# Order of the squares of x, the 64-row block product of two triangular inverses, and the queue of their transfers

## The chip, the cores and the metric

The kernel runs on one core of a Trainium2 chip. The metric is the device time of one execution in microseconds (us); for each kernel several executions are timed and the median is given. The engines of the core each work through their own list of instructions in order: PE (TensorE, matrix products), DVE (VectorE), ACT (ScalarE), POOL (GpSimd) and SP (SyncE, which here only starts transfers). ACT and POOL start transfers as well, and a transfer that an engine starts stands in that engine's list.

## The reference

One layer on x of 512 rows and 1024 columns, in float32: an RMS norm, one wide input projection, four parallel mixers (gated DeltaNet, RG-LRU, S5, RWKV-7), their output projections merged by sigmoid gates, an output projection, a squared-ReLU MLP and a last norm.

```python
h = _rmsnorm(x, norm1_g)
proj = h @ w_in
p_gdn, p_lru, p_s5, p_rwkv, p_gate = _split(proj, (GDN_COLS, LRU_COLS, S5_COLS, RWKV_COLS, GATE_COLS))
ys = (_gdn_mixer(p_gdn, ...), _rglru_mixer(p_lru, ...), _s5_mixer(p_s5, ...), _rwkv7_mixer(p_rwkv, ...))
for i in range(N_BRANCH):
    term = jax.nn.sigmoid(gate_logits[:, :, i]) * (ys[i] @ w_branch[i])
    merged = term if merged is None else merged + term
x = x + (merged @ w_out).astype(x.dtype)
h2 = _rmsnorm(x, norm2_g)
x = x + (jnp.square(jax.nn.relu(h2 @ mlp_w1)) @ mlp_w2).astype(x.dtype)
```

Two of the mixers are recurrences over time. The kernel computes both in chunks of 64 steps, and each needs the inverses of 32 unit triangular 64x64 matrices (4 heads by 8 chunks). These two sets of inverses are what the change is about: one for RWKV-7 (tiles whose names end in r) and one for the gated DeltaNet (names that end in g).

## The kernel before, in words

**Products.** A weight unit is 128 x 1024 numbers (512 KB). `unit` starts its transfer into a tile `raw` from SP's queue; ACT copies it to a rounded tile `hi` (L117), DVE computes `lo` = raw - hi (L120). `gemm` then makes 24 matrix products of 512 columns, three for each of eight slices of x: hi by the high part of x, hi by its low part, lo by its high part (L114). There are two tiles of `hi` and of `lo` and four of `raw`, so weights run a few units ahead of PE. The results stand in PSUM tiles called `acc`.

**Head.** `norm1` makes the high and low parts of each of the eight slices of x, scaled by the norm's weight: ACT writes the high part (L117, "split"), DVE the low part (L129). It then calls `norm_stat`, where ACT squares each slice (L117), DVE adds the squares up (L120), and PE sums over rows (`ssa`) and spreads the reciprocal root (`rsa`). While all this starts, PE runs `WARM` products of no use (`warm`); each counts as two passes in the trace.

**Order of the work.** A list of steps is given priorities, and a scheduler places every instruction on its engine's list by a timeline that it simulates. So a change of one step's instructions moves others around it. What the scheduler has written, the engines then execute in order, each instruction waiting for what it needs.

**The inverse.** `tri_inverse(nt, tf, nm)` runs once for r and once for g. `nt` holds 32 matrices of 64 rows. (1) It is written to memory in two transfers (L446) and read back in two (L450) with the 16x16 diagonal blocks laid out one to a partition. (2) DVE inverts those blocks in a loop of 15 steps of two operations each (L120, L459). (3) The inverses go to memory in four transfers, plain and transposed (L466), and come back in four (L470) as the tiles `a0t` and `tf`. Of the twelve transfers SP's queue starts six and ACT's six. (4) PE joins blocks of 16 to blocks of 32: `zp` is 64 products with a 16-row operand, ACT moves it to `zt` with one operation, `t1p` and `t2p` are 64 and 32 products, and ACT and DVE copy and add the results into place (L492, L494, L495). (5) PE joins blocks of 32 to blocks of 64 with `z2p` and `z3p`, 32 products each. The tile `tf` is then used by the recurrences.

**Around it.** `gdn_b` prepares the DeltaNet's decays: DVE copies the tile `pkT` out of PSUM, SP writes it to memory as `gscr` (L847), SP reads it back four times (L859, one tile that ACT then takes the exponential of), and ACT reads it back four more times (L853). `s5_y` reads the tile `scy` back with 16 transfers in ACT's list (L1344), ahead of a product called `glu`. The recurrences are chains of small products, `r`, `us`, `sn` and `oT`, between which ACT (L690, L691) and DVE (L124) move the results.

Of the kernel before, what the change touches and what calls it, by code (L numbers as in the profile page):

```python
# [11 lines left out]
ACT = mybir.ActivationFunctionType  # L12
# [85 lines left out]
RW0 = 1800  # L98
GATE0 = 2824
@with_exitstack  # L100
def trunk(ctx, tc, order, xT, wall, w8, prm, big, cst, gfr, out):
# [14 lines left out]
    def act(o, i, f, scale=1.0, bias=0.0):  # L116
        A.activation(out=o, in_=i, func=f, scale=scale, bias=bias)  # L117
# [181 lines left out]


    count = {"u": 0, "raw": 0}
    third = []

    def place(key):
        if key not in order:
# [10 lines left out]
    def unit(key, more=None, chain=None):  # L316

        u = count["u"]
        count["u"] += 1
        with priority(100 * u - (30000 if u else 50000)):  # L320
            k = u % (DEEP + len(third) // 2)
            if k < DEEP:
                hi, lo = (wp.tile([128, 1024], R, tag=f"{e}{k}", name=f"{e}{u}") for e in ("hi", "lo"))
            else:
                hi, lo = third
            if chain is None:
                raw = load(key)
            else:
                raw = chain
                (G if more is None else nc.sync).dma_start(out=raw, in_=wall[place(key)], **({"accum_op": ADD} if more is None else {}))  # L330
            if more is not None:
                G.dma_start(out=raw, in_=wall[place(more)], accum_op=ADD)
            act(hi, raw, ACT.Copy)
            tt(V, lo, raw, hi.bitcast(F), SUB)
        return v3(hi, 8), v3(lo, 8)

    def gemm(o, w, rh, rl, nk=8, k0=0, first=True, last=True):
        wh, wl = w
        n = 0
# [65 lines left out]

    def norm1():

        for k in range(8):
            split_g(xs[k], "g1", k, xgh[:, k, :], xgl[:, k, :])
        N1["rs"] = norm_stat(xs, "a")  # L410
        fr(xt)

    def proj(col):

        o = pa("acc")
        gemm(o, unit(("in", col)), xgh, xgl)
# [25 lines left out]
    def tri_inverse(nt, tf, nm):  # L442

        scr = tri_scr[nm]
        for par in range(2):
            (nc.sync, nc.scalar)[par].dma_start(  # L446
                out=flat(scr, 4160 * par, [[64, 64], [8320, 16], [1, 64]]), in_=nt[64 * par:64 * par + 64])
        nb, tn, tn2, tmp = (t1(n + nm) for n in ("nb", "tn", "tm", "tp"))
        for qe in range(2):
            (nc.sync, nc.scalar)[qe].dma_start(  # L450
                out=v3(nb, 16)[64 * qe:64 * qe + 64], in_=flat(scr, 1040 * qe, [[2080, 64], [64, 16], [1, 16]]))
# [12 lines left out]
        for qe in range(2):  # L464
            for s, t in ((0, tn3), (1, tm3)):
                (nc.sync, nc.scalar)[s].dma_start(  # L466
                    out=flat(tri_scr[nm, s], 1040 * qe, [[2080, 64], [64, 16], [1, 16]]), in_=t[64 * qe:64 * qe + 64])
        for par in range(2):
            for s, t in ((0, a0t), (1, tf)):
                (nc.sync, nc.scalar)[s].dma_start(  # L470
                    out=t[64 * par:64 * par + 64], in_=flat(tri_scr[nm, s], 4160 * par, [[64, 64], [8320, 16], [1, 64]]))
        fr(tn, tn2)

        zt, t11t, z2 = t1("zt" + nm), t2("t11t" + nm), t2("z2" + nm)
        zt3, t11, z23 = v3(zt, 16), v3(t11t, 16), v3(z2, 16)
        zp, t1p = ps("zp" + nm), ps("t1p" + nm)
        zp3 = v3(zp[:, 0:256], 16)
        t1p3, t2p3 = v3(t1p[:, 0:256], 16), v3(t1p[:, 256:512], 16)
        for x in range(16):
            for b in range(4):  # L480
                r0, c0 = 32 * b, 32 * (b % 2)
                mm(zp3[r0:r0 + 32, x, :], nt[r0:r0 + 16, x, c0:c0 + 32], a0t[r0:r0 + 16, x, c0:c0 + 16])
        act(zt, zp[:, 0:256], ACT.Copy, c_("hm")[:, 0:1])
        for x in range(16):
            for b in range(4):
                r0, c0 = 32 * b, 32 * (b % 2)
                mm(t1p3[r0:r0 + 16, x, :], zt3[r0:r0 + 32, x, :], tf[r0:r0 + 32, x, c0 + 16:c0 + 32])
                if b % 2 == 0:
                    mm(t2p3[r0:r0 + 32, x, :], tf[r0:r0 + 32, x, 0:32], zt3[r0:r0 + 32, x, :])
        for b in range(4):  # L490
            r0, c0 = 32 * b, 32 * (b % 2)
            A.copy(out=tf[r0:r0 + 16, :, c0 + 16:c0 + 32], in_=t1p3[r0:r0 + 16])  # L492
            if b % 2 == 0:
                tt(V, t11[r0:r0 + 32, :, 0:16], t2p3[r0:r0 + 32], a0t[r0:r0 + 32, :, 0:16], ADD)  # L494
                A.copy(out=t11[r0:r0 + 32, :, 16:32], in_=a0t[r0:r0 + 32, :, 16:32])  # L495
        fr(zt, t0t)

        z2p, z3p = ps("z2p" + nm), ps("z3p" + nm)
        z2p3, z3p3 = v3(z2p, 16), v3(z3p, 16)
        for x in range(16):  # L500
            for par in range(2):
                r0 = 64 * par
                mm(z2p3[r0 + 32:r0 + 64, x, :], nt[r0:r0 + 32, x, 32:64], t11[r0:r0 + 32, x, :])
        for par in range(2):
# [1324 lines left out]
```

## Time and profile before

| | |
|---|---|
| median of three runs | 880.21 us |
| the three runs | 877.97, 880.77, 880.21 us |
| the profiled execution's own time | 878.37 us |
| its span in the trace | 876.6 us |
| busy: PE, DVE, ACT, POOL | 852.6, 547.4, 427.2, 26.0 us |
| mean granted clock of TensorE | 0.988 |

A row of a timeline gives start and duration in us, the engine, the line of the kernel, the operation, and output and input by the program's names (tiles c, c0, c1a, c1b, c2, c3 are named storage places that many values pass through); in square brackets stands how long that engine had been idle just before, and what ended it. "x28" merges 28 instructions. A row of the waits gives the engine that waited, the tile, what it waited for, the total in us, the number of waits and the longest. A row of the windows gives, for a stretch from A to B, the busy time of PE, of its weight loads (PEld), DVE, ACT and POOL with their instructions, then the granted clock of TensorE, the busy share of the transfer engines and GB/s.

### The profile page before, as it was taken

Reading aid. Unit: us, or ns where it says so; the run is one execution under the profiler, and the core shown is the slowest. Engines: PE = TensorE matmul, PEld = TensorE weight load, DVE = VectorE, ACT = ScalarE, POOL = GpSimd, SP = SyncE. Lnnn points to the kernel's source line nnn. Section 1 sums busy time; section 2 is a strip of 40 time slices with the busy share of each in tenths; the row PEclk is TensorE's granted clock in tenths of the full one; section 3 lists DMA queues with packets and bytes.
Section 4 is the critical chain, followed back from the end, with each engine's and each line's share of the span. In section 5 each row is a group of like instructions: output and inputs, shape, how many; then the busy total and the mean of one; then the engine's idle time right before and its main releaser. Section 6 shows DMA issues by size and latency. Waiting matters only on the chain.

```text
span 876.6 us, 13021 instructions
## 1 busy us (share of the span) xinstructions
PE 852.6 (97%) x5175; PEld 683.9 (78%) x5175; DVE 547.4 (62%) x974; ACT 427.2 (49%) x600; POOL 26.0 (3%) x38
## 2 busy tenths in 40 slices
PE   8999999998999899999999999999999999999996
PEld 6777777777767677777888788888888888888885
DVE  6899796993676347845645652454437553868553
ACT  8735557954532254433523333765545443644433
POOL 1000000000000000000000000000100110010000
PEclk9999999998999899999999999999999999999998
DMA  8433345455365643344232232556676877463302
GB/s 298 134 114 104 109 117 111 105 148 147 111 182 155 163 144 111 107 119 136 73 106 99 75 130 96 192 145 174 164 195 165 239 170 194 164 137 104 120 25 96
DMA packets 79293, 119.97 MB, mean 137 GB/s; under 512 B 42544, under 2 KB 49392, under 8 KB 79216
## 3 DMA queue, kind: packets, MB, share of 16 engines
q1 hardware_dynamic: 51968, 100.40, 35.5%
q0 software_dynamic: 3456, 12.58, 8.5%
q10 hardware_dynamic: 23808, 6.16, 3.3%
q8 instruction: 40, 0.66, 0.3%
q14 instruction: 21, 0.17, 0.1%
HBM read 103.79 MB, written 13.17 MB: 133 GB/s over the span
## 4 chain that ended last, share of the span: by engine, by line
PE 80%; DVE 7%; DMA 6%; ACT 4%; issue 2%; ACTq 1%; SPq 1%; DVEq 0%
PE acc L114 24%; PE facc L114 20%; PE dacc L114 17%; PE oacc L114 5%; PE bacc L114 5%; DVE c L120 2%; DMA c1a<-scrg 1%; ACT c L117 1%; DVE lo L120 1%; PE s L114 1%; DVE c1a L120 1%; DVE c L129 1%; ACT L117 1%; DMA c1a<-gscr 1%; DMA scrg<-c1a 1%
## 5 line engine op out<-in xcount | busy, mean ns | idle before, releaser
L114 PE MATMUL acc<-c,hi 128*128 128x512 f32 x864 | 279.1, 401 | 3.1 <-DVE c L129 2.5
L117 ACT ACTIVATE hi<-raw 128x1024 fp32r<-128x1024 f32 x113 | 119.5, 1058 | 214.8 <-PE facc L114 73.5
L120 DVE TENSOR_TENSOR lo<-raw,hi 128x1024 fp32r<-128x1024 f32 x113 | 138.1, 1223 | 117.9 <-ACT hi L117 117.8
L114 PEld LDWEIGHTS acc<-c,hi 128*128 128x128 f32 x864 | 162.4, 191 | 43.2 <-DVE c L129 5.0
L114 PE MATMUL acc<-c,lo 128*128 128x512 f32 x432 | 175.1, 406 | 2.0 <-DVE lo L120 2.0
L114 PE MATMUL facc<-c,hi 128*128 128x512 f32 x336 | 103.4, 389 | 0.0
L114 PEld LDWEIGHTS acc<-c,lo 128*128 128x128 f32 x432 | 82.3, 190 | 21.9 <-DVE lo L120 3.1
L117 ACT ACTIVATE c<-c 128x512 f32<-128x512 f32 (+5 forms) x101 | 63.9, 638 | 19.3 <-DVE c L120 12.3
L114 PEld LDWEIGHTS facc<-c,hi 128*128 128x128 f32 x336 | 63.1, 188 | 13.0
L120 DVE TENSOR_TENSOR c<-c 128x16 f32<-128x16 f32 (+8 forms) x125 | 65.3, 537 | 5.1 <-ACT c L117 4.6
L114 PE MATMUL facc<-c,lo 128*128 128x512 f32 x168 | 65.5, 390 | 0.0
L114 PE MATMUL facc<-c,c1a 128*128 128x512 f32 x264 | 62.8, 391 | 0.0
L114 PE MATMUL dacc<-hi,c 128*128 128x512 f32 x176 | 57.4, 389 | 0.0
L117 ACT ACT_TABLE_LOAD x41 | 52.6, 1283 | 9.6 <-DMA c<-scu 3.7
L114 PEld LDWEIGHTS facc<-c,c1a 128*128 128x128 f32 x264 | 49.3, 188 | 10.2
L120 DVE TENSOR_TENSOR c1a<-raw,c1a 128x1024 fp32r<-128x1024 f32 x21 | 25.7, 1223 | 32.8 <-ACT c1a L117 32.7
L120 DVE TENSOR_TENSOR c<-acc,c 128x512 f32<-128x512 f32 x33 | 22.6, 688 | 36.3 <-PE acc L114 34.7
L114 PE MATMUL bacc<-c1a,hi 128*128 128x512 f32 x128 | 41.8, 408 | 0.3 <-DVE c L120 0.3
L117 ACT ACTIVATE c1a<-raw 128x1024 fp32r<-128x1024 f32 x21 | 22.2, 1059 | 36.6 <-PE facc L114 29.0
L114 PE MATMUL oacc<-c,hi 128*128 128x512 f32 x128 | 39.8, 392 | 0.1
L114 PEld LDWEIGHTS dacc<-hi,c 128*128 128x128 f32 x176 | 33.0, 188 | 6.9
L114 PEld LDWEIGHTS facc<-c,lo 128*128 128x128 f32 x168 | 31.5, 188 | 6.5
(394 smaller groups left out, 1187.2 us busy)
## 6 DMA issues: line engine op xcount, KB each, us to landing
raw<-in_wall_dram SPq DMA_DIRECT2D x134, 512.0 KB, 3.5
c<-in_wall_dram POOLq DMA_DIRECT2D x18, 512.0 KB, 5.8
c<-in_wall_dram SPq DMA_DIRECT2D x6, 512.0 KB, 3.5
raw<-in_wall_dram POOLq DMA_DIRECT2D x6, 512.0 KB, 6.2
scg<-c1b SPq DMA_DIRECT2D x11, 256.0 KB, 2.4
c<-scg SPq DMA_DIRECT2D x11, 256.0 KB, 4.2
c1b<-in_xT_dram SPq DMA_DIRECT2D x8, 256.0 KB, 5.4
c<-in_xT_dram SPq DMA_DIRECT2D x8, 256.0 KB, 4.8
```

Of the source, the lines that this page charges most:

```text
L114: P.matmul(out=o, lhsT=l, rhs=r, start=start, stop=stop)
L117: A.activation(out=o, in_=i, func=f, scale=scale, bias=bias)
L120: e.tensor_tensor(out=o, in0=a, in1=b, op=op)
L129: V.scalar_tensor_tensor(out=o, in0=a, scalar=s, in1=b, op0=op0, op1=op1)
```

## The change

Four edits.

1. `WARM` goes from 14 to 10.
2. `norm1` asks for the first two weight units before it splits x, and the squares are ordered behind the second unit's `hi` copy. `proj` takes those two units from a list.
3. All twelve transfers of an inverse are started from SP's queue.
4. Step (4) of the inverse handles both pairs of 16-blocks of a 64-row half at once. `zp` is 32 products with 64-row operands, 64 rows and 32 columns of result. `zt` is 64 columns wide per matrix, cleared by POOL, and filled by two ACT and two DVE operations. `t1p` is 32 products of the same shape; `t2p`, 32 products as before, follows them in a PSUM tile of its own. The tile `t11` and its two ACT copies are gone: the sum goes into `a0t` in place, and `z2p` reads `a0t`.

```diff
-WARM = 14
+WARM = 10
@@ unit
-            act(hi, raw, ACT.Copy)
+            high.append(A.activation(out=hi, in_=raw, func=ACT.Copy, scale=1.0, bias=0.0).ins)
@@ norm1, proj
+        early.extend(unit(("in", RW0 + 128 * m)) for m in (6, 7))
         for k in range(8):
             split_g(xs[k], "g1", k, xgh[:, k, :], xgl[:, k, :])
-        N1["rs"] = norm_stat(xs, "a")
+        with tc.issue_after(high[1]):
+            N1["rs"] = norm_stat(xs, "a")
...
-        gemm(o, unit(("in", col)), xgh, xgl)
+        gemm(o, early.pop(0) if early else unit(("in", col)), xgh, xgl)
@@ tri_inverse
-            (nc.sync, nc.scalar)[par].dma_start(
+            nc.sync.dma_start(
                 out=flat(scr, 4160 * par, [[64, 64], [8320, 16], [1, 64]]), in_=nt[64 * par:64 * par + 64])
...
-        for x in range(16):
-            for b in range(4):
-                r0, c0 = 32 * b, 32 * (b % 2)
-                mm(zp3[r0:r0 + 32, x, :], nt[r0:r0 + 16, x, c0:c0 + 32], a0t[r0:r0 + 16, x, c0:c0 + 16])
-        act(zt, zp[:, 0:256], ACT.Copy, c_("hm")[:, 0:1])
-        for x in range(16):
-            for b in range(4):
-                r0, c0 = 32 * b, 32 * (b % 2)
-                mm(t1p3[r0:r0 + 16, x, :], zt3[r0:r0 + 32, x, :], tf[r0:r0 + 32, x, c0 + 16:c0 + 32])
-                if b % 2 == 0:
-                    mm(t2p3[r0:r0 + 32, x, :], tf[r0:r0 + 32, x, 0:32], zt3[r0:r0 + 32, x, :])
+        zt, z2 = t4("zt" + nm), t2("z2" + nm)
+        G.memset(zt, 0.0)
+        def pairs(t, x, r0, o):
+            return t[r0:r0 + 64, x, :].rearrange("p (b c) -> p b c", b=2)[:, :, o:o + 16]
         for x in range(16):
+            for r0 in (0, 64):
+                mm(zp4[r0:r0 + 64, x], nt[r0:r0 + 64, x, :], pairs(a0t, x, r0, 0))
         for b in range(4):
             r0, c0 = 32 * b, 32 * (b % 2)
+            if b % 2:
+                ts(V, zt3[r0:r0 + 32, :, c0:c0 + 16], zp4[r0:r0 + 32, :, 1], hm[r0:r0 + 32, 0:1], MUL)
+            else:
+                act(zt3[r0:r0 + 32, :, c0:c0 + 16], zp4[r0:r0 + 32, :, 0], ACT.Copy, hm[r0:r0 + 32, 0:1])
+        for x in range(16):
+            for r0 in (0, 64):
+                mm(t1p4[r0:r0 + 64, x], zt3[r0:r0 + 64, x, :], pairs(tf, x, r0, 16))
+        for x in range(16):
+            for r0 in (0, 64):
+                mm(t2p3[r0:r0 + 32, x, :], tf[r0:r0 + 32, x, 0:32], zt3[r0:r0 + 32, x, 0:16])
+        for b in range(4):
+            r0, c0 = 32 * b, 32 * (b % 2)
+            A.copy(out=tf[r0:r0 + 16, :, c0 + 16:c0 + 32], in_=t1p4[r0:r0 + 16, :, b % 2])
             if b % 2 == 0:
-                tt(V, t11[r0:r0 + 32, :, 0:16], t2p3[r0:r0 + 32], a0t[r0:r0 + 32, :, 0:16], ADD)
-                A.copy(out=t11[r0:r0 + 32, :, 16:32], in_=a0t[r0:r0 + 32, :, 16:32])
+                tt(V, a0t[r0:r0 + 32, :, 0:16], t2p3[r0:r0 + 32], a0t[r0:r0 + 32, :, 0:16], ADD)
...
-                mm(z2p3[r0 + 32:r0 + 64, x, :], nt[r0:r0 + 32, x, 32:64], t11[r0:r0 + 32, x, :])
+                mm(z2p3[r0 + 32:r0 + 64, x, :], nt[r0:r0 + 32, x, 32:64], a0t[r0:r0 + 32, x, 0:32])
```

The scheduler writes the lists anew. Three places follow. In the rows, a number behind a name is a tile's running number, and the lines behind `norm_stat` are a few higher in the changed kernel.

The head, ACT's list, the last splits and squares before: a split (`c0`, from x in `c1b`) and a square (`c3`, `c1a`, `c2`) alternate, and the second unit's `hi1` comes behind all of them.

```order
L117 ACTIVATE c3_79<-c1b_77 128x512
L117 ACTIVATE c0_75<-c1b_77,pr_81 128x512
L117 ACTIVATE c1a_76<-c1b_77 128x512
L117 ACTIVATE c0_75<-c1b_77,pr_81 128x512
L117 ACTIVATE c3_79<-c1b_77 128x512
L117 ACTIVATE c0_75<-c1b_77,pr_81 128x512
L117 ACTIVATE c2_78<-c1b_77 128x512
L117 ACTIVATE hi1_214<-raw1_216 128x1024
```

The same place now: eight splits, `hi1`, and then the eight squares.

```order
L333 ACTIVATE hi0_113<-raw0_115 128x1024
L117 ACTIVATE c0_75<-c1b_77,pr_81 128x512 x8
L333 ACTIVATE hi1_119<-raw1_121 128x1024
L117 ACTIVATE c3_79<-c1b_77 128x512 x5
L117 ACTIVATE c1a_76<-c1b_77 128x512
L117 ACTIVATE c3_79<-c1b_77 128x512
L117 ACTIVATE c2_78<-c1b_77 128x512
```

The squares have moved behind `hi1`; DVE's list has moved with it (all eight low parts, then `lo1`, then the sums).

The inverse of r, ACT's list, before: the transfers L470 and the copies L495 stand ahead of the four copies of `t1pr` (L492), and the exponential of the decays (`c1a_76<-c1a_76 128x1024`, with its table load) behind them.

```order
L470 DMA c2_78<-scrr1_170 64x16x64 x2
L117 ACTIVATE c1b_77<-c1b_77 128x512
L495 COPY c3_79<-c2_78 32x16x16 x2
L117 ACTIVATE hi25_2481<-raw25_2483 128x1024
L691 COPY c3_79<-c3_79 64x256
L492 COPY c2_78<-t1pr_1634 16x16x16 x4
L117 ACT_TABLE_LOAD
L117 ACTIVATE c1a_76<-c1a_76 128x1024
```

The same place now:

```order
L117 ACT_TABLE_LOAD
L117 ACTIVATE c1a_76<-c1a_76 128x1024
L981 COPY c3_79<-c2_78 64x256
L1355 DMA c3_79<-scy_1552 16x8x64 x13
L702 COPY c1b_77<-c3_79 64x256 x2
L1355 DMA c3_79<-scy_1552 16x8x64
L504 COPY c2_78<-t1pr_1667 16x16x16 x4
L702 COPY c1b_77<-c3_79 64x256
L1355 DMA c3_79<-scy_1552 16x8x64 x2
```

The exponential and fourteen of the sixteen transfers of `scy` now stand ahead of the copies of `t1pr`.

The inverse of g, DVE's list, before: the result of `us` is moved out of PSUM (`us_2653`) ahead of the loop over the 16-blocks, whose first operation is the one on 128x1.

```order
L120 TENSOR_TENSOR c3_79<-s1g_2009,c1a_76 64x2x2x64 x2
L124 TENSOR_SCALAR c1b_77<-us_2653 64x256
L120 TENSOR_TENSOR lo31_3186<-raw31_3187,hi31_3185 128x1024
L120 TENSOR_TENSOR c1b_77<-sn_2659,c3_79 64x256
L120 TENSOR_TENSOR c3_79<-c1b_77,wc_251 64x256
L120 TENSOR_TENSOR c1b_77<-acc_3116,c3_79 128x512
L120 TENSOR_TENSOR c1a_76<-c2_78,c1a_76 128x1
L459 TENSOR_REDUCE c2_78<-c1a_76 128x1
```

The same place now:

```order
L120 TENSOR_TENSOR lo31_3060<-raw31_3061,hi31_3059 128x1024
L120 TENSOR_TENSOR c1a_76<-c2_78,c1a_76 128x1
L461 TENSOR_REDUCE c2_78<-c1a_76 128x1
L120 TENSOR_TENSOR c1a_76<-c2_78,c1a_76 128x2x2
L461 TENSOR_REDUCE c2_78<-c1a_76 128x2
L120 TENSOR_TENSOR c1a_76<-c2_78,c1a_76 128x3x3
L461 TENSOR_REDUCE c2_78<-c1a_76 128x3
L120 TENSOR_TENSOR c1a_76<-c2_78,c1a_76 128x4x4
L461 TENSOR_REDUCE c2_78<-c1a_76 128x4
L120 TENSOR_TENSOR c1a_76<-c2_78,c1a_76 128x5x5
L124 TENSOR_SCALAR c1b_77<-us_2496 64x256
```

The first operation of the loop waits for the transfers L452; a step of the recurrence (`us_2496`) now stands behind it, after nine operations of the loop.

More of the change, by code (lines that the diff above doesn't have):

```diff
@@ L301, in trunk @@
     count = {"u": 0, "raw": 0}
-    third = []
+    third, high, early = [], [], []
     def place(key):
@@ L449, in tri_inverse @@
         for qe in range(2):
-            (nc.sync, nc.scalar)[qe].dma_start(
+            nc.sync.dma_start(
                 out=v3(nb, 16)[64 * qe:64 * qe + 64], in_=flat(scr, 1040 * qe, [[2080, 64], [64, 16], [1, 16]]))
@@ L465, in tri_inverse @@
             for s, t in ((0, tn3), (1, tm3)):
-                (nc.sync, nc.scalar)[s].dma_start(
+                nc.sync.dma_start(
                     out=flat(tri_scr[nm, s], 1040 * qe, [[2080, 64], [64, 16], [1, 16]]), in_=t[64 * qe:64 * qe + 64])
@@ L469, in tri_inverse @@
             for s, t in ((0, a0t), (1, tf)):
-                (nc.sync, nc.scalar)[s].dma_start(
+                nc.sync.dma_start(
                     out=t[64 * par:64 * par + 64], in_=flat(tri_scr[nm, s], 4160 * par, [[64, 64], [8320, 16], [1, 64]]))
         fr(tn, tn2)
[L474 to L478, printed above, removed]
@@ L490, in tri_inverse @@
+        G.memset(zt, 0.0)
+        zt3, z23 = v3(zt, 16), v3(z2, 16)
+        hm = c_("hm")
+        zp = ps("zp" + nm)
+        zp4 = v4(zp, 16, 2)
+        def pairs(t, x, r0, o):
+            return t[r0:r0 + 64, x, :].rearrange("p (b c) -> p b c", b=2)[:, :, o:o + 16]
+        for x in range(16):
+            for r0 in (0, 64):
+                mm(zp4[r0:r0 + 64, x], nt[r0:r0 + 64, x, :], pairs(a0t, x, r0, 0))
         for b in range(4):
             r0, c0 = 32 * b, 32 * (b % 2)
-            A.copy(out=tf[r0:r0 + 16, :, c0 + 16:c0 + 32], in_=t1p3[r0:r0 + 16])
+            if b % 2:
+                ts(V, zt3[r0:r0 + 32, :, c0:c0 + 16], zp4[r0:r0 + 32, :, 1], hm[r0:r0 + 32, 0:1], MUL)
+            else:
+                act(zt3[r0:r0 + 32, :, c0:c0 + 16], zp4[r0:r0 + 32, :, 0], ACT.Copy, hm[r0:r0 + 32, 0:1])
@@ new lines, in tri_inverse @@
+        t1p, t2p = ps("t1p" + nm), ps("t2p" + nm)
+        t1p4, t2p3 = v4(t1p, 16, 2), v3(t2p[:, 0:256], 16)
+        for x in range(16):
[7 more added lines that the diff above has]
+            A.copy(out=tf[r0:r0 + 16, :, c0 + 16:c0 + 32], in_=t1p4[r0:r0 + 16, :, b % 2])
@@ L493, in tri_inverse @@
             if b % 2 == 0:
-                tt(V, t11[r0:r0 + 32, :, 0:16], t2p3[r0:r0 + 32], a0t[r0:r0 + 32, :, 0:16], ADD)
-                A.copy(out=t11[r0:r0 + 32, :, 16:32], in_=a0t[r0:r0 + 32, :, 16:32])
-        fr(zt, t0t)
+                tt(V, a0t[r0:r0 + 32, :, 0:16], t2p3[r0:r0 + 32], a0t[r0:r0 + 32, :, 0:16], ADD)
+        fr(zt)
         z2p, z3p = ps("z2p" + nm), ps("z3p" + nm)
@@ L519, in tri_inverse @@
                 A.copy(out=tf[r0:r0 + 32, :, 32:64], in_=z3p3[r0:r0 + 32])
-        fr(t11t, z2)
+        fr(t0t, z2)
     def split_y(y, nm):
```

## The prediction

> **What bounds the kernel now.** I read the page first, for the share of each engine.
>
> ```profile
> span 876.6 us, 13021 instructions
> ...
> PE 852.6 (97%) x5175; PEld 683.9 (78%) x5175; DVE 547.4 (62%) x974; ACT 427.2 (49%) x600; POOL 26.0 (3%) x38
> ...
> PEclk9999999998999899999999999999999999999998
> ```
>
> PE is busy for 852.6 of 876.6 us. So the change can move the time in three ways only: by PE's idle 24.0 us, by the stretches in which PE's clock is lowered (the eights in the row of clocks: two stretches near 200 and 300 us, and the end), and by the work that PE is given. The waits of PE come next, since they say where the 24.0 us lie.
>
> ```profile
> PE t1pr L114 <- issue: 2.9, 1, 2.9
> PE zpg L114 <- DMA c1a<-scrg: 2.6, 2, 1.4
> PE acc L114 <- DVE c L129: 2.5, 6, 0.8
> ...
> PE glu L114 <- ACT c L117: 1.5, 1, 1.5
> PE us L114 <- ACT c1b L690: 1.1, 1, 1.1
> ...
> PE vtT L894 <- DVE egl L871: 0.7, 1, 0.7
> ```
>
> One of these rows is the head (2.5, the low parts of x). Five, 8.8 us in sum, lie around the two inverses: in the products of r, in the products of g, and in what shares ACT and DVE with them. The windows show the clock there, and the stretch of the head beside one in which PE has no gap.
>
> ```profile
> 0.00:25.00 25.00, 20.99 (x94) 16.07 (x95) 17.58 (x69) 20.40 (x36) 2.89 (x11) 1.00 0.86 281
> 25.00:50.00 25.00, 25.00 (x110) 18.58 (x110) 23.12 (x94) 15.88 (x21) 0.00 (x0) 1.00 0.42 128
> ...
> 195.00:200.00 5.00, 3.10 (x173) 2.47 (x172) 1.14 (x2) 0.00 (x0) 0.00 (x0) 0.97 1.05 233
> 200.00:205.00 5.00, 4.01 (x30) 3.40 (x30) 0.83 (x2) 1.45 (x4) 0.00 (x0) 0.50 0.68 137
> 205.00:210.00 5.00, 5.00 (x27) 4.08 (x27) 0.89 (x2) 3.50 (x4) 0.00 (x0) 0.85 0.07 20
> ...
> 290.00:295.00 5.00, 2.09 (x27) 1.35 (x27) 0.32 (x1) 2.66 (x5) 0.00 (x0) 1.00 1.19 271
> 295.00:300.00 5.00, 5.00 (x140) 4.59 (x141) 2.67 (x5) 1.16 (x3) 0.00 (x0) 0.53 0.75 256
> 300.00:305.00 5.00, 5.00 (x19) 3.84 (x17) 0.00 (x0) 0.82 (x1) 0.00 (x0) 0.79 0.19 70
> 305.00:310.00 5.00, 5.00 (x213) 4.26 (x213) 2.34 (x4) 1.33 (x5) 0.00 (x0) 0.89 0.36 108
> ```
>
> 25.00 us over 110 products is 0.227 us for each: the price of a gemm's product in all that follows. After each of the two stretches in which PE is half idle (195 and 290) the granted clock falls to about 0.5 and comes back over some ten microseconds. As (1 - clock) x 5 us that is 2.5 + 0.75 after the first, 2.35 + 1.05 + 0.55 after the second: 7.2 us. So the middle loses 8.8 + 7.2 = 16.0 us, and that is all that the inverses' edits can win back.
>
> **The head.** The timeline of the first 25 us, on the three engines:
>
> ```profile
> 0.89 5.40 PE L114 MATMUL warm<-one 128*128 128x128 f32 x28 [0.89 <-POOL one L289]
> ...
> 5.09 1.06 ACT L117 ACTIVATE hi<-raw 128x1024 fp32r<-128x1024 f32 x1 [3.07 <-DMA raw<-in_wall_dram]
> ...
> 6.05 0.71 ACT L117 ACTIVATE c<-c1b,pr 128x512 fp32r<-128x512 f32 x1
> ...
> 6.67 0.62 ACT L117 ACTIVATE c<-c1b 128x512 f32<-128x512 f32 x1
> ...
> 6.81 0.50 PE L114 MATMUL acc<-c,hi 128*128 128x512 f32 x1 [0.53 <-ACT c L117]
> ...
> 7.32 1.41 DVE L129 SCALAR_TENSOR_TENSOR c<-c1b,pr,c 128x512 fp32r<-128x512 f32 x2
> ...
> 9.91 0.69 DVE L120 TENSOR_TENSOR c<-c 128x512 f32<-128x512 f32 x1
> ...
> 24.38 0.83 PE L114 MATMUL rsa<-cs,sta 128*128 128x128 f32 x6
> ```
>
> Between 6.81 and 24.38 us PE made 52 products (35 + 17 by hi and lo in the groups of this window) and `ssa`. At 0.227 the 52 take 11.8 us, `ssa` about 1.0: 12.8 of 17.6 us, so 4.8 us are lost. The cause is the alternation: a split and a square together take 1.25 us on ACT (7.32 less 6.05 on either engine's clock), a low part and a sum 0.70 + 0.69 on DVE, and each pair feeds only three products, 0.68 us.
>
> After the change eight splits run at 0.62 us from 6.05 to 11.0, eight low parts at 0.70 from 7.32 to 12.9. PE needs 5.5 us for the first gemm and the last low part leaves its last two products: end about 13.4. `hi1` is done at 12.1, `lo1` (1.2 us, behind the low parts) at 14.1; the second gemm starts by hi and loses 0.3 us on lo. It ends near 19.2. The squares run from 12.1 to 17.1, the sums behind `lo1` to about 19.0, so `ssa` and four more products end near 21. That is 3.4 us earlier than 24.38; 0.4 I keep for the third unit's `hi2`, which now stands behind the squares. Bounds: 0 (as under the warm-up rival) to 4.8. **Head: -3.0.** What comes late next is `rs`; the scaled results wait for it, but six accumulators stand open at that time, 33 us of products.
>
> Cutting the warm-up shortens nothing by itself: it ends at 6.29 us and the first product waits for the first split. It ends near 5.3 after the change.
>
> **PE's work in the inverses.** The trace counts two passes for each of these products.
>
> ```profile
> 173.36 1.23 PE L114 MATMUL zpr<-c,c1a 16*32 16x16 f32 x124
> ...
> 209.94 1.19 PE L114 MATMUL z2pr<-c,c1a 32*32 32x32 f32 x62
> ...
> 254.68 1.59 PE L114 MATMUL s1g<-c 64*64 64x128 f32 x32
> ```
>
> A pass is 9.9 ns in `zpr` (four row groups in turn), 19 ns in `z2pr` (two), 50 ns in `s1g` with four times the columns. Before: 128 passes of `zp` and 192 of `t1p` and `t2p`, 320 x 9.9 = 3.2 us. After: 64 + 64 + 64; the new products use two row groups and 32 columns, as `z2pr` does, so 192 x 19 = 3.65 us. **+0.45 an inverse, +0.9 for both.** Ends: 192 x 9.9 = 1.9 us (-2.6 for both) and 128 x 50 + 64 x 19 = 7.6 us (+8.8); the row of the same two row groups and columns decides. The page "TensorEngine Tiling (Array Packing)" of the Trainium skill, section Instruction Overhead, gives each product about 60 cycles however few columns it has. By it 96 products instead of 160 would take 0.6 of 3.2 us, -1.3 an inverse, and the forecast would come out 3.5 us lower, 877.6. The 9.9 ns against the 19 ns above disagree with it.
>
> Clearing `zt` is POOL's, idle there, and hidden; the four evictions of `zp` instead of one cost ACT and DVE two short operations each, and lie beside gemm products. The two L495 copies that go cost ACT more than their 0.4 us in g: they waited for transfers, and `us` of the recurrence stood behind them (the 1.1 us of the waits). That wait goes; so should the 2.6 us of `zpg`, since PE's list now holds more gemm products between the last transfer and `zpg`.
>
> **The transfers on SP's queue, g.** These rows carry the chain from the finished `nt` to DVE's loop:
>
> ```profile
> 258.20 0.85 DVE L120 TENSOR_TENSOR c<-s1g,c1a 64x256 f32<-64x256 f32 x2
> ...
> 259.08 0.62 SPq L446 DMA_DIRECT2D scrg<-c1a  x1
> ...
> 264.84 0.58 SPq L450 DMA_DIRECT2D c1a<-scrg  x1
> ...
> 270.71 0.16 DVE L120 TENSOR_TENSOR c1a<-c,c1a 128x1 f32<-128x1 f32 x1 [5.29 <-DMA c1a<-scrg]
> ```
>
> From 259.05 to 270.71 are 11.7 us, through writing and reading. On one queue each pair is issued one behind the other: +0.6, since reading starts when both are written, and the second reading another 0.6 later: 12.3 to 12.9 us. Before, DVE stood idle for 5.29 of it and nobody minded: the result of `us` had been moved out already, and PE had gemms. Now `us_2496` is queued behind the loop's first nine operations, and PE's `sn` waits for it. From the last `s1g` to `sn` PE's list holds 42 gemm products (9.5 us), one `r` and one `us` (16 passes of 50 ns at most, 0.8): 10.3. The chain takes 1.3 (the last adds, 0.85 and one more) + 12.6 + 1.8 (nine operations, the first 0.16) + 0.4 = 16.1. PE waits 5.8 us; with queues less full, down to 0; take 5.0. **g: idle 5.0 + 0.7 left over, before 3.7.**
>
> **The inverse of r.** Here ACT's list decides. Rows of the timeline, and at the end one of the issues of transfers (count, size of each, median us to landing):
>
> ```profile
> 198.49 5.47 SPq L859 DMA_DIRECT2D c1a<-gscr  x4
> ...
> 202.39 0.75 ACT L492 COPY c<-t1pr 16x256 f32<-16x256 f32 x2 [0.48 <-DVE c L120]
> ...
> 206.47 1.28 ACT L117 ACT_TABLE_LOAD   x1 [2.48 <-DMA c1a<-gscr]
> 207.77 1.06 ACT L117 ACTIVATE c1a<-c1a 128x1024 f32<-128x1024 f32 x1
> ...
> 219.07 3.79 PE L114 MATMUL s5y<-c 128*128 128x64 f32 x32
> ...
> 230.99 2.72 ACTq L1344 DMA_DIRECT2D c<-scy  x6
> ...
> scrg<-c1a ACTq DMA_DIRECT2D x2, 64.0 KB, 3.3
> ```
>
> The exponential waited until 206.47 for the four readings of `gscr`, 8.0 us after the first was issued. Before, the copies of `t1pr` stood ahead of it, now behind it and behind fourteen transfers of `scy` at 0.45 us each (2.72 for six): 6.3 us. The chain from `pkT`: copy and issue 1.0, landing of `gscr` about 3.3 (as the writes of 64 KB in the list of issues), readings 8.0, table and exponential 2.3, transfers 6.3, four copies and two like them 2.2: 23.1 us to `z2pr`. PE's list holds between: 42 gemm products (9.5), 16 products of `s5y` (32 passes, 3.8), `zpr`, `t1pr` and `t2pr` (3.6), six `vtT` (under a gemm product each, 1.1): 18.0. PE waits up to 5.1 at `z2pr`; take 3.5, as SP's queue is emptier there than at 198 us (transfer engines at 1.05). Behind it `glu` waits for its GELU, which needs the last two transfers and a table load (about 3 us against 1.2 of `z2pr`): 2.0. Then `z3pr` waits for a DVE copy queued behind a multiplication that needs the readings of L864, issued by ACT after that: 0 to 5, take 1.5. **r: idle 7.0 (0 to 13), before 5.1.** The 2.9 us of "issue" in `t1pr` fell in a run of 192 short passes; there are 64 now, so I let it go.
>
> **Sum.** Idle of the middle 7.0 + 5.7 = 12.7 instead of 8.8; two lowered stretches as before, since both new gaps are as long as the old. So +3.9. Against the profiled execution's 878.37: -3.0 + 0.9 + 3.9 = +1.8, 880.2. That execution lies 1.84 under the median of the runs; half of it on top gives **881.1 us**. 0.3% (2.6 us) is about what a measurement here can tell from no change: the forecast is no change, own range 877 to 886.
>
> The page "TensorE: Matmul & The Clock Gate" of the Trainium skill, in its section "Why this matters for your kernels", says that an idle gap over about 3 us brings the slow clock back. The rows agree (2.89 us idle, then 0.50); by it a gap of 5 at `sn` would cost one such stretch, which the sum has.
>
> **Rivals.**
>
> *Cover holds, faster (0.33).* The lists are full of gemm products, and my chains take the transfers at the time of the fullest queues (1.05 and 1.19 of the engines' share in the windows of 195 and 290). With landings a third shorter, the wait at `sn` falls to 1, those of r to 4, and only one stretch is lowered (3.3): 8.3 instead of 16.0, -7.7. With head and work: 868.6, and as a median about 870. For it: DVE's 5.29 us of idling at this very loop left no row among the waits of PE. Against it: PE then had gemms that did not hang on DVE, and now has 10.3 us of them for a chain of 16.1.
>
> *ACT blocked at full length, slower (0.18).* The copies of `t1pr` behind the exponential and the transfers decide as soon as `gscr` lands later than PE's 18.0 us allow. At the upper ends, r 13.0 and g 6.3, with a third lowered stretch of 3.3 because r's gaps lie apart: 19.3 + 10.5 = 29.8 against 16.0, +13.8. With -3.0 and +0.9: 890.1.
>
> *The warm-up is too short (0.06).* PE is idle from 5.3 to 6.8. If the clock is not released by then, the first products run at half speed: eight at twice 0.227 are 1.8 us, and the gap costs more if the release slips a second time. Head 0 instead of -3.0: 884. In the window 0 to 25 the clock stands at 1.00 in the mean, which speaks against it. The same page of the Trainium skill, Part 1, asks for about 3.4 us of steady work, seen through a window that runs freely; by it 4.4 us of warm-up would mostly do.
>
> *The block product buys no PE time (within the forecast).* If passes cost 9.9 ns, the sum falls by 3.5, and stays in the forecast's range.
>
> **How the numbers follow.** Forecast 0.43 (of it 0.03 faster, 0.25 same, 0.15 slower), cover 0.33 (faster), ACT blocked 0.18 (slower), warm-up 0.06 (0.03 same, 0.03 slower). Faster 0.36, same 0.28, slower 0.36. The range leaves out a part of the first rival's low end and of the second's high end: 868.5 to 889.
>
> **What would show it.** Head: `rsa` near 21 us instead of 24.4, and no wait of `acc` for L129 over 0.3 us each. r: a wait of `z2pr` for DVE or ACT, of `glu` for ACT, ACT's 4 copies of `t1pr` behind L1355. g: a wait of `sn` for DVE around 265 to 280 us, none of `zpg` for a transfer. PE's busy time near 853.5 less the head's hidden part. It is wrong if the middle has no gap over 2 us (then about 870) or if a gap sits where I named none.

## The result, and the profile after

The changed kernel takes 875.55 us (median of 8 runs, 871.29 to 876.90) beside 880.36 us before (8 runs, 875.73 to 881.57): a ratio of 0.995, 95% interval 0.9928 to 0.9973. It is faster by half a per cent, where I had forecast no change. The profiled executions say 873.1 us of span after 876.6.

The busy times and the clock of the page after:

```profile
span 873.1 us, 12499 instructions
...
PE 854.0 (98%) x4911; PEld 688.6 (79%) x4911; DVE 549.3 (63%) x978; ACT 425.1 (49%) x597; POOL 28.3 (3%) x40
...
PEclk9999999997999999999999999999999999999998
```

PE has 264 passes fewer and is busy 1.4 us longer. Its waits now:

```profile
PE sn L114 <- DVE c1b L124: 2.2, 1, 2.2
PE zpr L114 <- DMA c<-scrr: 2.1, 1, 2.1
...
PE acc L114 <- ACT c L117: 1.2, 1, 1.2
PE r L114 <- DVE c L120: 1.0, 1, 1.0
...
PE acc L114 <- DVE c L129: 0.8, 1, 0.8
PE glu L114 <- ACT c L117: 0.7, 1, 0.7
PE us L114 <- ACT hi L333: 0.5, 1, 0.5
```

The 2.9 us of issue in `t1pr` and the 2.6 us of `zpg` are gone, and `us` waits 0.5 us for ACT instead of 1.1. In the head the 2.5 us for the low parts have become 0.8; the wait of the first product for its split has grown from 0.5 to 1.2 us, since the warm-up ends earlier. New are the waits of `sn` (which I had named) and of `zpr` for its transfers (which I had not). `z2pr` and `z3pr`, for which I had priced 5.0 us, do not wait at all.

The head, on PE and ACT:

```profile
0.89 4.30 PE L114 MATMUL warm<-one 128*128 128x128 f32 x20 [0.89 <-POOL one L289]
6.38 0.51 PE L114 MATMUL acc<-c,hi 128*128 128x512 f32 x1 [1.20 <-ACT c L117]
20.56 0.95 PE L114 MATMUL ssa<-one,c 128*128 128x1 f32 x8
27.63 1.05 PE L114 MATMUL rsa<-cs,sta 128*128 128x128 f32 x8
```
```profile
7.33 4.22 ACT L117 ACTIVATE c<-c1b,pr 128x512 fp32r<-128x512 f32 x6 [0.39 <-DMA c1b<-in_xT_dram]
12.14 1.06 ACT L333 ACTIVATE hi<-raw 128x1024 fp32r<-128x1024 f32 x1 [0.59 <-DMA raw<-in_wall_dram]
13.11 2.70 ACT L117 ACTIVATE c<-c1b 128x512 f32<-128x512 f32 x5
```

The splits run without squares between them and `hi1` starts at 12.14. The end of the second gemm comes earlier: the 48th gemm product in the trace starts at 19.9 us, before at 23.2. Since `ssa`, 1.0 us, has moved from before that product to behind it, the 52nd is the fairer mark, with `ssa` done in both: 21.7 against 24.2, so 2.5 us earlier. `rsa` I had looked for near 21 us; it comes at 27.6, since PE's list holds more gemm products ahead of it. No wait of PE for it stands in the list, as the prediction's cover for `rs` assumed.

To compare kernels I split each profiled span in three: PE's idle time up to 850 us; the time at half clock up to 850 us, by the trace's records of the clock, of which half is lost; and the rest, which is PE's work at full clock with the end behind 850 us. Where PE idles at half clock the split counts that time twice, so the rest is good to about 2 us. In e6 and e11 the first record of the clock comes only at 13.6 and 13.3 us, and two gemm products ahead of it take 1.05 us where they take 0.62 behind it; so the 7.1 and 6.5 us from the first gemm product to that record are counted as half clock. Each span is of one execution, which lay up to 4.7 us (e7) from its kernel's median.

```
kernel                  median   span    idle head / 150-350 / other   half clock   rest
before                  880.4   876.6       4.0  /  12.2   /  0.4         17.1      851.4
changed                 875.6   873.1       2.9  /   8.8   /  0.4         20.5      850.7
e1 head only            869.6   867.5       3.2  /   8.2   /  0.4         17.1      847.1
e2 queue only           884.0   884.7       3.9  /  11.7   /  2.3         30.7      851.5
e3 block product only   884.3   885.3       3.2  /   7.9   /  1.5         34.1      855.6
e4 changed, WARM 14     872.7   872.9       2.5  /  10.7   /  0.4         13.7      852.4
e5 head and queue       882.2   880.4       3.0  /  16.7   /  0.4         30.7      844.9
e6 head and product     872.6   870.8       2.4  /  10.9   /  0.4         13.9      850.2
e7 head, WARM 14        874.1   877.0       2.9  /  14.9   /  0.4         20.5      848.6
e9 last sum on POOL     883.4   884.5       5.2  /  13.8   /  1.3         27.3      850.7
e10 head, sum on POOL   893.7   889.1       3.5  /  21.4   /  3.0         30.7      845.9
e11 WARM 10 only        879.6   877.0       3.2  /  11.8   /  0.4         27.0      848.0
e12 queue and product   877.3   874.7       4.1  /   8.9   /  0.6         13.7      854.3
```

Before against changed: idle 16.6 to 12.1, -4.5; half clock 17.1 to 20.5, +1.7; rest -0.7; together -3.5, the difference of the spans. The new stretch at half clock is the one of the head, 3.4 us. In the middle both kernels have 17.1 us of it. In all six kernels with `WARM` at 10 the first gemm runs in part at half clock (3.4 us, in e6 and e11 some 7), in none of the seven with 14.

### The profile page after: what moved, and what is told of

It reads as the page before. It is cut to its first block, busy times and chain, and to the rows that moved or that the text cites. A ratio compares the mean times of both kernels' runs of the same rounds, so it can differ in the third digit from the quotient of the medians.

```text
span 873.1 us, 12499 instructions
## 1 busy us (share of the span) xinstructions
PE 854.0 (98%) x4911; PEld 688.6 (79%) x4911; DVE 549.3 (63%) x978; ACT 425.1 (49%) x597; POOL 28.3 (3%) x40
## 4 chain that ended last, share of the span: by engine, by line
PE 81%; DVE 7%; DMA 4%; ACT 4%; SPq 2%; issue 1%; ACTq 1%; DVEq 0%
PE acc L114 25%; PE facc L114 20%; PE dacc L114 17%; PE bacc L114 5%; PE oacc L114 5%; DVE c L120 2%; DVE lo L120 1%; DMA scg<-c1b 1%; ACT L117 1%; PE s L114 1%; DVE c1a L120 1%; DVE c1b L120 1%; DVE c L129 1%; ACTq L1355 1%; SPq L1247 1%
## 5 line engine op out<-in xcount | busy, mean ns | idle before, releaser
L114 PE MATMUL acc<-c,lo 128*128 128x512 f32 x432 | 172.7, 401 | 1.9 <-DVE lo L120 1.8
L114 PEld LDWEIGHTS acc<-c,lo 128*128 128x128 f32 x432 | 82.2, 190 | 23.0 <-DVE lo L120 3.9
```

What stands on the lines that cost most here:

```text
L114: P.matmul(out=o, lhsT=l, rhs=r, start=start, stop=stop)
```

## The experiments

The ratios below are against runs of the kernel before on the same chip (medians 877.8 to 878.7).

**e1 to e3: each part alone.** e1 takes the diff's hunks for WARM, `unit`, `norm1` and `proj`; e2 replaces the pairs of queues in `tri_inverse`; e3 takes the hunk behind `fr(tn, tn2)`.

```diff
# e1
+        with tc.issue_after(high[1]):
+            N1["rs"] = norm_stat(xs, "a")
# e2
-            (nc.sync, nc.scalar)[par].dma_start(
+            nc.sync.dma_start(
# e3
-                mm(zp3[r0:r0 + 32, x, :], nt[r0:r0 + 16, x, c0:c0 + 32], a0t[r0:r0 + 16, x, c0:c0 + 16])
+                mm(zp4[r0:r0 + 64, x], nt[r0:r0 + 64, x, :], pairs(a0t, x, r0, 0))
```

> The kernel before with the head's edits alone (WARM 10, the two early weight units, the squares behind the second unit's hi copy); the inverses as before. Theory A, the parts add up: the head gives 2.5 to 3 us (876.6 less 2.5 to 3 in the span, first gemm ended near 13.5 us instead of 23), the waits of zpg for transfers (2.6) and of us for ACT (1.1) stay. Theory B, the head is paid back by the slow clock after the short warm-up and by rsa being later: no change within 1 us, and the gain of the whole change lies in the middle. Theory C, the order of the lists decides: the time may come out anywhere within 4 us, and gaps appear in the middle that the kernel before does not have.

> The kernel before with the twelve transfers of each inverse started from SP's queue, nothing else. Theory A: ACT's list is freed of six issues of 0.6 us and of waiting for them; PE's waits in r and g fall by up to 3 us, the time by 0 to 3. Theory B: most of the change's gain (3 to 4 us) shows here. Theory C: anything within 4 us, with gaps at new places.

> The kernel before with the block product alone (both pairs of blocks at once, t11 and its ACT copies gone), transfers on both queues as before. Theory A: a pass of the new products is 29 to 30 ns instead of 8 to 10, PE gets 1.9 us more work for each inverse, 3.8 in all; the waits of us for ACT (1.1) go: slower by 1 to 4 us. Theory B: faster by 2 to 4 us, since the run of 192 short passes with its gap of 2.9 us is gone. Theory C: anything within 4 us.

Measured: e1 869.63 us, ratio 0.9896 (0.9868 to 0.9923); e2 884.02 us, 1.0061 (1.0037 to 1.0086); e3 884.33 us, 1.0057 (1.0034 to 1.0080). The head's edits alone do twice as well as the whole change, and each edit of the inverse alone makes the kernel slower. Theory A had the signs of e1 and e3, and no size: the head gave 9 us where its own stretch explains 3 to 4. Theory B fell. Theory C was right that anything may come out, but its bound of 4 us was passed in all three.

Most of e1's gain is in the middle: in the table its idle time and half of its slow time fall by 5.7 us there, everything else by 3.4. The longest waits of e1 (the third, behind the splits, is in the head):

```profile
PE us L114 <- DVE c1b L691: 1.7, 2, 1.5
PE bacc L114 <- DVE c L120: 1.6, 1, 1.6
PE acc L114 <- ACT c L117: 1.5, 1, 1.5
...
PE r L114 <- issue: 1.3, 1, 1.3
```

The code of the inverses is that of the kernel before. Yet `zpg` waits 0.4 us instead of 2.6, and `t1pr` not at all instead of 2.9. What differs there is the order: the scheduler has written all of the middle anew, and the first `zpr` stands at 201.5 us, before at 170.5.

**e4: WARM back at 14 in the changed kernel.** Every list is otherwise the same, row for row.

```diff
-WARM = 10
+WARM = 14
```

> The changed kernel with WARM back at 14. Theory A: the half-speed stretch from 8.0 to 11.4 us of the changed kernel comes from the gap of 1.2 us behind the shorter warm-up, and goes: 1 to 1.7 us faster than the changed kernel, the clock at 1.00 in the first 25 us. Rival: PE's stalls between the first products (each 0.8 us) bring that stretch anyway, or the lists come out in another order: within 0.5 us of the changed kernel.

Measured: 872.72 us, 0.9930 (0.9907 to 0.9952), beside 0.9950 (0.9928 to 0.9973) for the changed kernel: the intervals overlap, so a gain over 10 is not shown. The half-clock stretch of the head is gone. What e4 shows beyond that is the inverse of r, which PE passes at full clock here:

```profile
204.87 2.05 PE L114 MATMUL zpr<-c,c1a 64*64 64x32 f32 x62
224.04 1.20 PE L114 MATMUL z2pr<-c,c1a 32*32 32x32 f32 x64 [1.91 <-ACT c L504]
228.78 3.78 PE L114 MATMUL glu<-c,c1a 128*128 128x512 f32 x4 [3.54 <-ACT c L117]
```

The same rows of the changed kernel:

```profile
207.12 3.62 PE L114 MATMUL zpr<-c,c1a 64*64 64x32 f32 x62 [2.08 <-DMA c<-scrr]
228.52 1.20 PE L114 MATMUL z2pr<-c,c1a 32*32 32x32 f32 x64
230.38 1.98 PE L114 MATMUL glu<-c,c1a 128*128 128x512 f32 x4 [0.66 <-ACT c L117]
```

With the same lists, what is a wait of 1.9 and 3.5 us in one kernel is a slow `zpr` and a wait for transfers in the other.

**e5 and e6: two parts of three.** e5 is the changed kernel with the old products, e6 the changed kernel with the old pairs of queues.

```diff
# e5: e1 with
-                (nc.sync, nc.scalar)[s].dma_start(
+                nc.sync.dma_start(
# e6: the changed kernel with
-                nc.sync.dma_start(
+                (nc.sync, nc.scalar)[s].dma_start(
```

> The changed kernel with the old products of the inverses: the head's edits and the twelve transfers on SP's queue. Theory A, the block product is what the changed kernel pays with (3.8 us of PE work and more time at the slow clock): 868 to 871 us, close to the head alone. Theory B, the queue edit costs 5 us whatever stands beside it, as it did alone: near 875.

> The changed kernel with the transfers of the inverses on both queues: the head's edits and the block product. Theory A: near the changed kernel, 874 to 877, since the product's 3.8 us of PE work and its slow stretches stay. Theory B, the product and the queue help each other (ACT's list is free while the product's evictions need it): 878 or more, worse than the changed kernel.

Measured: e5 882.2 us, 1.0045 (1.0025 to 1.0065); e6 872.56 us, 0.9950 (0.9927 to 0.9974). The queue costs 1.5% on top of the head alone, and nothing on top of the head with the product (e6 against the changed kernel, both 0.995). For e5 both theories failed. For e6 theory A was right that it comes out as the changed kernel does, though its range begins 1.4 us above the time; theory B failed. There is no one price of "the queue" that fits both.

**e7: the head without the shorter warm-up**, lists as in e1 but for the warm-up.

```diff
-WARM = 10
+WARM = 14
```

> The head's edits without the shorter warm-up, the inverses as before. Theory A: 1 to 3 us faster than the head alone (869.6), 867 to 869, since the slow stretch at 8.5 to 11.9 us goes, as it did with 14 in the changed kernel. Rival: the slow stretches of the middle move against the products with every shift of the start, and the median stays within 1 us of 869.6.

Measured: 874.06 us, 0.9954 (0.9931 to 0.9977), slower than e1, and clear of its interval. So the same one-number edit that tended to help the changed kernel costs 4 us here. The stretch at 8.6 to 12.0 us goes, as theory A says, but the idle time of the middle rises from 8.2 to 14.9 us, 3.0 of it at `t1pg` for issue; the profiled execution of e7 took 878.79 us, though, its kernel's slowest, so the idle time of a usual one is likely less. The rival's mechanism, a shift of the start against the clock and the transfers, fits but is not shown; its size (within 1 us) was wrong. Which of the two makes the gaps was not tried.

**e8: PE alone.** Runs of 70 big products with runs of small ones between them (the calls of the new kernel, here on one line and without the mixed run at the end).

```diff
+    gemms(70); four(512); gemms(70); two64(170); gemms(70); two32(270); gemms(70)
...
```

> Not the kernel: PE alone, data random, nothing to wait for. 70 products of 128x128 by 512 columns, then 512 products with a 16-row operand in four row groups (as zp before), 70, 170 products of 64x64 by 32 columns in two halves (as zp and t1p now), 70, 270 products of 32x32 by 32 (as z2p), 70, then 170 of the 64x64 kind with two big products after every eight, and 70. The output is not the reference's. Theory A: a pass takes 8 to 10 ns, 29 to 30 ns and 18 to 19 ns in the three kinds, and in each of these runs of 5 to 10 us without a gap the granted clock falls to 0.5 within about 7 us, while in the mixed run it stays at 1.0: small products alone bring the slow clock. Rival, only idling brings it: the clock stays at 1.0 throughout, and what the inverses lose they lose by their gaps.

The timeline, each run of small products with the issue gaps in it:

```profile
22.72 2.19 PE L34 MATMUL four<-s 16*32 16x16 f32 x241
26.96 1.90 PE L34 MATMUL four<-s 16*32 16x16 f32 x128 [2.04 <-issue]
30.69 1.90 PE L34 MATMUL four<-s 16*32 16x16 f32 x128 [1.82 <-issue]
...
64.11 10.11 PE L34 MATMUL two<-s 64*64 64x32 f32 x340
...
90.24 3.12 PE L34 MATMUL two<-s 32*32 32x32 f32 x185
94.14 7.08 PE L34 MATMUL two<-s 32*32 32x32 f32 x256 [0.78 <-issue]
```

and the clock in the three kinds (the third number from the end):

```profile
26.00:32.00 6.00, 3.22 (x227) 3.11 (x229) 0.00 (x0) 0.00 (x0) 0.00 (x0) 0.51 0.03 5
...
64.00:69.00 5.00, 5.00 (x169) 4.89 (x168) 0.00 (x0) 0.00 (x0) 0.00 (x0) 1.00 0.01 3
69.00:74.00 5.00, 5.00 (x179) 5.00 (x176) 0.00 (x0) 0.00 (x0) 0.00 (x0) 1.00 0.01 3
...
90.97:94.39 3.42, 2.64 (x166) 2.56 (x162) 0.00 (x0) 0.00 (x0) 0.00 (x0) 1.00 0.02 5
94.39:97.80 3.41, 3.41 (x133) 3.31 (x128) 0.00 (x0) 0.00 (x0) 0.00 (x0) 0.50 0.02 5
97.80:101.21 3.41, 3.41 (x128) 3.29 (x124) 0.00 (x0) 0.00 (x0) 0.00 (x0) 0.50 0.02 5
```

Three things follow. The prices of a pass were about as theory A had them: 2.19/241 = 9.1 ns, 10.11/340 = 29.7 ns, and 3.12/185 = 16.9 ns, a little under its 18 to 19. The 16-row kind keeps its price for some 240 passes only; then PE is fed 128 passes each 3.5 to 3.7 us. And the clock falls in the 16-row and 32-row kinds, not in the 64-row kind, which ran for 10 us at full clock, nor in the mixed run. Theory A was wrong for the 64-row kind: it had the slow clock in all three. The rival is not ruled out as to what starts the slow clock, since in both falling kinds PE had stood idle for issue in the 3.4 us before (1.2 and 0.8 us of them). It does not explain what follows: from 94.39 to 101.21 the 32-row kind ran without a gap, and the clock stayed at 0.50.

**e9 and e10: a small move that writes the lists anew.** The last of the seven sums of squares runs on POOL, in the kernel before (e9) and in e1 (e10).

```diff
-            tt(V, accs[-2], accs[-2], accs[-1], ADD)
+            tt(G if parts == 1 else V, accs[-2], accs[-2], accs[-1], ADD)
```

> The kernel before with one operation moved: the last of the seven sums of squares, 128x512, runs on POOL and not on DVE. By itself it can cost or save no more than 1 us (POOL is idle there, the result comes a little later), but the scheduler writes some 730 rows of PE's list in another order. Theory C, the order of the lists between 150 and 330 us decides: the time differs from the kernel before by 2 to 6 us either way, by other gaps and slow stretches there, while the first 150 us stay within 1 us. Theory A, edits act by their own cost: within 1 us of the kernel before, 877 to 880.

> The same move in the kernel with the head's edits alone. Theory A, the head's edits give 9 us by themselves: 868.5 to 871. Theory C, they give 2.5 to 3.5 us in the first 150 us and the rest was the order that the scheduler happened to write: the first 150 us as in the head alone, the time anywhere between 868 and 878, nearer to 875.

Measured: e9 883.41 us, 1.0051 (1.0024 to 1.0077); e10 893.74 us, 1.0174 (1.0141 to 1.0208), 24 us above e1.

In e9 the move is not neutral, and the run says little of the order. POOL needs 2.79 us for the addition, PE waits for it at `ssa`, and the clock is at half from 19.2 to 26.0 us:

```profile
16.00 2.79 POOL L120 TENSOR_TENSOR c<-c,c 128x512 f32<-128x512 f32 x1 [12.57 <-DVE c L120]
18.84 1.59 PE L114 MATMUL ssa<-one,c 128*128 128x1 f32 x8 [1.47 <-POOL c L120]
```

The 48th gemm product starts at 27.8 us, before at 23.2: 4.6 us are lost in the head of the profiled execution, where theory C had said that the first 150 us stay within 1 us, and that is about the whole difference of the medians, 4.7. So e9 does not show theory C; it fits theory A's principle, that an edit acts by its own cost, at a price that theory A had within 1 us.

In e10 the move is neutral where it is made. At 98 us e10 and e1 are still within half a microsecond of one another: the last `b8T` ends at 98.2 and 98.7. Nearly all of the difference arises at 150 to 350 us, and in e10 the windows and the two largest waits show it (e1 has PE busy for 97.6 of the same 100 us, e10 for 82.2):

```profile
150.00:175.00 25.00, 21.60 (x101) 16.91 (x100) 24.50 (x75) 18.36 (x26) 0.12 (x1) 1.00 0.35 90
175.00:200.00 25.00, 20.65 (x204) 16.68 (x203) 15.43 (x24) 10.37 (x14) 0.00 (x0) 0.86 0.81 162
200.00:225.00 25.00, 21.69 (x411) 18.53 (x410) 5.99 (x13) 5.76 (x10) 0.00 (x0) 0.80 0.27 66
225.00:250.00 25.00, 18.28 (x124) 13.54 (x124) 16.09 (x27) 12.51 (x17) 0.00 (x0) 0.80 0.47 127
```
```profile
PE acc L114 <- ACT hi L333: 5.8, 5, 2.1
PE us L114 <- DVE c L519: 5.3, 1, 5.3
```

This is theory C, and larger than I had put it: one small move in the head, with the same work to do, is worth 24 us by the order of the lists. It rests on this one pair of kernels.

**e11: WARM 10 alone**, lists of the kernel before. The edits of `norm1` are in it, with the squares ordered behind the first unit's `hi`, which moves no row.

```diff
-WARM = 14
+WARM = 10
```

> The kernel before with WARM at 10 and every list otherwise the same, row for row. Theory A: the clock falls in the head as it did with 10 in the changed kernel, 0 to 1.7 us slower than before. Rival: PE's work before the first product is not on the path and the slow stretches merely move: within 1 us of before.

Measured: 879.55 us, 1.0014 (0.9990 to 1.0038): no change is shown, and 0.9 us lies in the ranges of both. The trace has theory A's slow clock and the rival's price. The first row is from e11, the second the same place before:

```profile
9.13 1.05 PE L114 MATMUL acc<-c,hi 128*128 128x512 f32 x2
8.70 0.62 PE L114 MATMUL acc<-c,hi 128*128 128x512 f32 x2
```

Up to 13.3 us the products run at half speed, and yet `ssa` starts at 17.25 us, before at 17.26: in the old head PE waits for a split and a low part every 1.25 us anyway, and the slow products fill that wait.

**e12: both edits of the inverses**, the head as before. Beside the lines shown it has the block product of e3.

```diff
-                (nc.sync, nc.scalar)[s].dma_start(
+                nc.sync.dma_start(
```

> Both edits of the inverses without the head's. Theory A, each part has its own price (queue +5.4, product +5.0 alone): 886 to 890. Theory C: anything from 875 to 888; with the head's edits the same two gave 875.55, so by a head of 3 us alone it would be about 878.5.

Measured: 877.26 us, 0.9985 (0.9965 to 1.0005), no change. Alone the two edits cost 0.6% each, together nothing, so theory A's sum fails. Against this kernel the head's edits of the changed kernel give 0.9950/0.9985, some 3 us, with intervals that overlap: here theory C's 878.5 and the head's own 3 us fit.

The eight corners of the three edits, as ratios, in one place:

```
                      products as before         block product
                     both queues   SP queue    both queues   SP queue
head as before         1.0000       1.0061       1.0057       0.9985
head's edits           0.9896       1.0045       0.9950       0.9950
```

## Why the prediction was wrong

**The head, -3.0: right, and of the right size.** The 52nd gemm product is 2.5 us earlier. In the table the head's edits take 3.9 to 4.6 us off the rest (means of groups with equal products, e11 left out since its slow products fill waits: 851.2 to 846.6, 855.0 to 851.1) and about 1 us off the head's idle; the half-clock stretch at 8.1 to 11.5 us gives 1.7 back. That stretch is the rival "the warm-up is too short", which came true with a price of 1.7 us in this execution; by the 7.1 us of e6 it can be 3.5.

**PE's work in the inverses, +0.9: mis-sized.** The row that I took for the new products, `z2pr`, has two row groups and 32 columns as they do, but 32 rows where they have 64. The trace after has this row for them:

```profile
220.27 2.05 PE L114 MATMUL t1pr<-c,c1b 64*64 64x32 f32 x62
```

A pass is 2.05 us over 62, 33 ns, where I had 19; `t2pr`, with 32 rows, takes 18.6 ns (1.19 us over 64). So an inverse takes 128 x 33 + 64 x 18.6 = 5.4 us and not 3.65, +2.2 and not +0.45, and both +4.4. In the table the block product adds 3.8 and 4.5 us to the rest. The gap for issue that I let go is gone, as the prediction said: none of the kernels with the block product has a gap for issue among the waits of PE, and all with the old products have one (2.9 us at `t1pr` before, 3.0 at `t1pg` in e7, 0.9 to 2.8 at the longest in the others).

**The middle's waits, +3.9: the step that failed.** Idle between 150 and 350 us fell from 12.2 to 8.8, and I had it rise. Two faults of different kind lie in it.

In r the chain was right to 0.2 us and the cover was not. I had 23.1 us from `pkT` to the copies of `t1pr`. The trace after:

```profile
199.04 4.71 SPq L472 DMA_DIRECT2D c<-scrr  x3
...
215.41 1.28 ACT L117 ACT_TABLE_LOAD   x1 [1.21 <-DMA c1a<-gscr]
...
218.01 5.28 ACTq L1355 DMA_DIRECT2D c<-scy  x11
...
224.48 1.11 ACT L504 COPY c<-t1pr 16x256 f32<-16x256 f32 x3
```

`pkT` ended at 202.7, the copies at 225.6: 22.9 us. But PE came to `z2pr` at 228.5 and not at 220.6, since `zpr` had waited 2.1 us for its transfers, where the prediction named no gap (their last three issues, L472, took SP's queue 4.71 us, and 3.08 in e4, which has the same lists and no such wait), and a stretch of ten microseconds at half clock lay on the way. I had added slow clock and waits, as if each came on top of the other. Against a chain of fixed length they cover one another; e4, with the same lists at full clock, shows the waits of 1.9 and 3.5 us that the prediction had priced at 3.5 and 2.0.

In g the mechanism was right and the size was not: `sn` waits for DVE behind the loop, 2.2 us where I took 5.0. The rows after:

```profile
252.13 0.85 DVE L120 TENSOR_TENSOR c<-s1g,c1a 64x256 f32<-64x256 f32 x2
...
262.06 0.16 DVE L120 TENSOR_TENSOR c1a<-c,c1a 128x1 f32<-128x1 f32 x1 [4.71 <-DMA c1a<-scrg]
```

252.98 to 262.06 are 9.1 us for writing and reading, on one queue, where the two queues of before had taken 11.7. The added 1.2 us for the single queue did not show; the transfer engines were emptier over that stretch (a busy share of 0.62, before 0.77), which fits but was not tried by itself. That is nearly the condition of the rival "cover holds" (landings a third shorter), to which I had given 0.33. Its time, about 870, was missed as well: it had one lowered stretch in the middle, and there are 17.1 us at half clock.

**The slow clock: the sum came true, the reading behind it did not.** I took the lowered clock of the kernel before for two stretches, each brought by PE's idling, and the 2.89 us of idling near 200 us for a sign that a gap of about 3 us is needed. The records of the clock show three stretches: 199.7 to 206.5, 295.3 to 302.1 and 308.9 to 312.3 us. The first begins while PE has idled for 1.6 of the 3.4 us before, and the third behind 3.4 us without a gap, full of short products of g. In the changed kernel the four stretches up to 850 us begin behind 1.0 to 2.1 us of idling in 3.4. That the middle has 17.1 us of slow clock before and after, as the forecast assumed, is luck: e3 has 34.1 and e4 13.7.

**What the parts could not have told.** The eight corners show no price for a part that holds in every pair, beyond the head's 3 us and the product's 4 that the split finds. The same queue edit costs 13 us in one set of lists and nothing in another. So even with the right waits the forecast would have needed a range of both signs; what was wrong was to take "no change" for the likeliest. Why the scheduler's order in the changed kernel is a good one is explained only as far as its gaps can be listed; of e10's poor one only the two largest waits are shown, not what in the order makes them.

## What to carry to other kernels

Where a scheduler writes the lists, an edit has two effects: its own, which can be worked out, and the new order of everything behind it, which cannot be read from the diff; test each part alone and in pairs, and move something harmless as a control before a part gets the credit, with a look at its own place: e10's move was harmless there, e9's cost 4.6 us. Here the best kernel is the head's edits alone (0.9896), though e10 shows how much of that hangs on one order, and the block product and the queue should be left out or tried with other orders. A wait is priced against where the waiting engine really stands at that time: delays on both sides cover one another and are not to be summed. Take the price of a product from a row with the same rows, columns and row groups, or time that shape by itself.

## What the runs showed of the hardware

Small products can bring the slow clock without any gap. In e3 the window of 3.4 us before its slow stretch is full of `t1pr` and `t2pr`:

```profile
197.80:201.22 3.42, 3.42 (x127) 3.23 (x126) 0.10 (x1) 0.61 (x2) 0.00 (x0) 1.00 1.01 250
201.22:204.63 3.41, 3.41 (x16) 2.96 (x15) 0.73 (x2) 1.96 (x6) 0.00 (x0) 0.50 0.76 143
```

PE is busy for all of it, and the clock still falls. The kernel before does the same at 308.9 us, and e9 at 316.1, each behind 3.4 us with no gap and over 200 passes, most of them of `t1pg`:

```profile
305.49:308.90 3.41, 3.41 (x206) 3.04 (x203) 1.71 (x3) 0.49 (x2) 0.00 (x0) 1.00 0.40 107
```

It is no rule: in e2 the stretch from 193.09 to 196.50 us has 199 passes, most of `t1pr`, and the clock stays at 1.00. The page "TensorE: Matmul & The Clock Gate" of the Trainium skill, Part 1, lays the slow clock to idle windows; the rows of e3 go further than that. In e8 the 64-row kind kept full clock for 10 us, so by that run alone the new `t1pr` would not do it; whether `t2pr` or the zeros in `zt` make the difference was not tried.

Very short products have a second limit. In e8 the 16-row kind ran at 9.1 ns for 241 passes and then at 128 passes in 3.45 to 3.73 us, 27 to 29 ns each, PE waiting for issue: in a long run they are no faster than passes of four times the rows. The clock was at 0.50 from 26.1 us on, but the first of these waits began at 24.9, at full clock.

Runs of one and the same kernel differ with the clock. Of the runs of e1 the one with the highest granted clock, 0.997, took 867.68 us, the one with the lowest, 0.984, 873.26 us; of the kernel before, 0.992 took 873.36 and 0.982 took 880.96.
